# Two pools of slots re-divided: attention keys into the second pool, merged sums allocated at their first write

## The chip, the cores and the metric

The kernel runs on one core of a Trainium2 chip. The core's engines run side by side, each through its own queue of instructions in a fixed order: TensorE (PE in the profile, with its weight loads as PEld), VectorE (DVE), ScalarE (ACT), GpSimd (POOL), and SyncE (SP), which issues the transfers from memory. An instruction that has to wait holds up all that stand behind it on its engine. The metric is the device time of the run in microseconds; lower is better.

## The reference

Two transformer blocks run one after the other over 512 tokens of width 1024, batch 1, in fp32. The second block has two layers, and the change is in its mixing part, which four branches share. Cut to what matters:

```
h = rmsnorm(x); z = h @ w_in          # split: q, k, v of each branch, and 4 x 1024 gates
yA = forgetting_attention(qA, kA, vA, fA)    # 8 heads of 64, causal; logits + F[q] - F[k]
yB = dsa_attention(...)               # each query keeps its 128 best keys of an index score
yC = retention(...);  yD = sliding_window_gqa(...)
branch_n = y_n @ w_branch[n]          # 512 -> 1024
merged = sum over n of sigmoid(gates_n) * branch_n
x = x + merged @ w_out;  then a gated feed-forward layer
```

## The kernel before

Activations stand transposed, features on the 128 partitions and the 512 tokens along the row, so that a 1024-wide tensor is eight tiles of 128x512. fp32 products are made of three matmuls of rounded parts (mm3, L186 to L188): high by high, low by high, high by low. A weight block is loaded as `raw`, ACT rounds it to `hi` (L166), DVE subtracts to `lo` (L111). A product with 1024 inputs is 24 matmuls into one of four PSUM banks tagged `mm`; scores and transposes take three banks tagged `sc`, the product of probabilities and values one bank `pv`. A bank is free again when an engine has read it out.

SBUF tiles come from pools of equal slots of 128x512 fp32. `g` (L95) has 48 slots (NSLOT). `g2` (L100; its tiles are called h in the trace) has 12 (NSLOT2). A tile that is allocated while all slots are taken waits for the last reader of an older tile, so an instruction's first write to it can wait for an engine that has nothing to do with its data.

In `mix2` the slots of g2 go to `va`, the values of forgetting attention (4), to the eight tiles of `merged`, which are allocated ahead of everything else, and later to `vc` (4). In `fox_pair` each of four pairs of heads takes eight tiles of g: q, q2, k and k2, two each. Their scores are two matmuls each (L1116, L1117).

A pair's attention is a generator (`attend`) over four blocks c of 128 queries: scores on PE, mask and negative maximum on DVE (L1000), exponential on ACT (L123), reciprocal and scaling on DVE (L1012, L1014), transposes on PE (L1025), copies on ACT (L1028), and after the four blocks the product with the values on PE (L1039). The four pairs of forgetting attention, then four of the sparse branch (scores at L1128, L1129) stand in one list, `bg`; `pump` moves the first of them on by one step between two pieces of other work. A second list holds `select`, which finds the best 128 keys: 16 rounds of two DVE instructions (L1162, L1163) for each of three blocks, then L1168 makes the mask.

`branch` makes eight products of the gates (`gate(d)`, 24 matmuls each). A gate's bank is read out by a multiply on DVE (L111, out<-in `h<-psmm,g`) into `merged[d]` for the first branch, into a temporary tile for the others. With lead 4, gates 0 to 3 come first. Then the attention of the branch is drained, and the products with `w_branch` (12 matmuls for each of eight banks) take turns with gates 4 to 7. What is written is not what runs: a scheduler re-orders the program by priorities and free slots, and sets each engine's fixed order ahead of time.

Of the kernel before, what the change touches and what calls it, by code (L numbers as in the profile page):

```python
# [10 lines left out]
F32R = mybir.dt.float32r  # L11
# [9 lines left out]
KT = D // P  # L21
# [50 lines left out]
class Builder:  # L72
# [1017 lines left out]
    def fox_pair(self, ys, pair, pq, pk, va):  # L1090
        nc, ap = self.nc, self.ap
        tq, tk = self.tmp(), self.tmp()
        self.mul(tk, pk, self.rb)
        self.mul(tq, pq, self.rb)


        q, k = [self.g(F32R) for _ in range(2)], [self.g(F32R) for _ in range(2)]
        q2, k2 = [self.g(F32R) for _ in range(2)], [self.g(F32R) for _ in range(2)]
        hg, f0 = pair // 2, pair % 2 * 64
        fq, fk = self.fq[hg], self.fk[hg]  # L1100
        for i in range(2):
            r, o = slice(i * 64, i * 64 + 64), slice(64 - i * 64, 128 - i * 64)
            mine, other = 64 - i * 64 + i * 32, 64 - i * 64 + 32 - i * 32
            nc.scalar.copy(k[i][r], tk[r])
            nc.scalar.copy(k[i][o], tk[r])
            self.sub(k2[i][r], tk[r], k[i][r].bitcast(F32))
            nc.gpsimd.memset(k2[i][other:other + 32].bitcast(F32), 0.0)
            nc.scalar.copy(k2[i][mine:mine + 32], fk[f0 + i * 32:f0 + i * 32 + 32].bitcast(F32))
            nc.scalar.copy(q[i][r], tq[r])
            self.sub(q[i][o], tq[r], q[i][r].bitcast(F32))  # L1110
            nc.scalar.copy(q2[i][r], tq[r])
            nc.scalar.copy(q2[i][o], fq[f0:f0 + 64].bitcast(F32))

        def score(i, c, ps, k0, nk):
            qs = slice(c * P, (c + 1) * P)
            nc.tensor.matmul(ps, q[i][:, qs], k[i][:, k0:k0 + nk], start=True, stop=False)  # L1116
            nc.tensor.matmul(ps, q2[i][:, qs], k2[i][:, k0:k0 + nk], start=False, stop=True)  # L1117

        return self.attend(ys, pair, score, self.maskc, lambda i: 3e38,
                           lambda i, b: va[b][:, pair * P + i * 64:pair * P + i * 64 + 64],  # L1120
                           lambda c: list(range(c + 1)))
# [152 lines left out]
    def branch(self, l, n, y, x, first, gens=(), lead=3):  # L1274


        nc = self.nc
        gs = []

        def gate(d):  # L1280
            bk = self.bank("mm")
            self.gemm_b(bk, self.weights(self.I["w_gates"][l, n, d], KT * P), x)
            g = self.merged[d] if first else self.tmp()
            self.mul(g, bk, self.rb)
            self.act(g, g, AF.Tanh, scale=0.5)
            gs.append(g)
            self.pump(self.rate)

        for d in range(lead):
            gate(d)  # L1290
        self.drain(*gens)
        wb = None
        for d in range(KT):
            if d + lead < KT:
                gate(d + lead)
            if d % 2 == 0:
                wb = self.weights(self.I["w_branch"][l, n, d // 2], 1024)
            bb = self.bank("mm")
            self.gemm_b(bb, wb, [y[j] for j in range(4)], off=(d % 2) * 512)
            g = gs[d]  # L1300
            nc.vector.scalar_tensor_tensor(g, g, 1.0, bb, ALU.add, ALU.mult)
            if not first:
                self.add(self.merged[d], self.merged[d], g)
            self.pump(self.rate)
# [33 lines left out]
    def mix2(self, l):  # L1338
# [11 lines left out]
        self.cosR, self.sinR = self.g(), self.g()  # L1350
        self.mul(self.cosR, self.cload("cos"), self.rb)
        self.mul(self.sinR, self.cload("sin"), self.rb)
        self.merged = [self.g2() for d in range(KT)]
        proj = lambda n: self.rope(self.project(wr[n], x), self.tmp())

        hh, ll = self.stack_k(self.rope(b0, self.tmp()))
# [57 lines left out]
        for c in range(CHUNKS):  # L1414
            g = sg[c]
# [6 lines left out]
        q, k = [], []  # L1422
# [211 lines left out]
```

## Time and profile before

| | us |
|---|---|
| median of 3 runs (lowest, highest) | 3044.45 (3042.66, 3047.03) |
| profiled execution, own time | 3042.95 |
| its span, first to last instruction | 3041.1 |
| PE busy | 2962.3 |
| DVE busy | 1995.9 |

PE is busy for 97% of the span, so what can be saved or lost is mostly in its few idle stretches and in the stretches where its granted clock is below full. The clock has two levels, 1.2 and 2.4 GHz; the mean granted over the run is 0.989 of full. The mixing parts of the two layers lie at about 960 to 1600 us and 2020 to 2640 us, and the work that the change touches at about 1060 to 1180 and 2100 to 2220.

### The profile page before, as it was taken

The numbers are of one execution on the slowest core, as the hardware profiler recorded it, in microseconds if no ns is written. First come the engines' busy times: TensorE is split into PE (matmuls) and PEld (weight loads), VectorE is DVE, ScalarE is ACT, GpSimd is POOL, SyncE is SP. The second block draws the span as 40 slices with busy tenths as digits, with TensorE's granted clock in tenths as the row PEclk, the third lists the DMA queues.
The fourth block names the chain that finished last, engine by engine and source line by source line (L and its number), as shares of the span: only waits on it lengthen the run. The fifth ranks groups of instructions, "written<-read, shape, count | busy, mean of one in ns | idle before, by whom it ended". The sixth has DMA issues, their size and how long they took to land.

```text
span 3041.1 us, 38875 instructions
## 1 busy us (share of the span) xinstructions
PE 2962.3 (97%) x14882; PEld 2463.9 (81%) x14882; DVE 1995.9 (66%) x3866; ACT 1354.9 (45%) x2279; POOL 113.7 (4%) x148
## 2 busy tenths in 40 slices
PE   8999899999999998999999999999899999999998
PEld 7887888888888877887888888888687788888887
DVE  7888664545447796556666566659866467675575
ACT  5523443422226565545244333356655453343343
POOL 0000000011010000000000001000000000010010
PEclk9999999999999999999999999999999999999999
DMA  5224442233324221222243333332122222323322
GB/s 172 84 91 105 123 164 93 86 94 94 102 85 132 87 70 49 63 87 87 63 132 97 97 91 103 102 121 84 42 70 69 81 80 84 125 92 102 97 93 82
DMA packets 98395, 287.12 MB, mean 94 GB/s; under 512 B 12161, under 2 KB 20609, under 8 KB 98209
## 3 DMA queue, kind: packets, MB, share of 16 engines
q1 hardware_dynamic: 95744, 283.07, 30.1%
q10 hardware_dynamic: 2464, 1.57, 0.3%
q8 instruction: 117, 1.92, 0.3%
q14 instruction: 70, 0.57, 0.1%
HBM read 274.67 MB, written 9.93 MB: 94 GB/s over the span
## 4 chain that ended last, share of the span: by engine, by line
PE 90%; DVE 7%; ACT 2%; DMA 1%; issue 1%; ACTq 0%; SPq 0%; DVEq 0%
PE psmm L186 27%; PE psmm L187 27%; PE psmm L188 27%; PE pspv L1039 2%; PE pssc L1025 1%; DVE g L111 1%; DVE lo L111 1%; DVE g L1163 1%; DVE m L1162 1%; PE pssc L1128 1%; DVE tmp L111 1%; DVE prob L1000 1%; PE pssc L1129 1%; PE pspv L824 0%; PE pssc L792 0%
## 5 line engine op out<-in xcount | busy, mean ns | idle before, releaser
L186 PE MATMUL psmm<-g,hi 128*128 128x512 f32 (+1 forms) x3456 | 1342.9, 391 | 17.2 <-DVE h L111 6.4
L188 PE MATMUL psmm<-g,lo 128*128 128x512 f32 (+1 forms) x3456 | 1344.1, 390 | 3.5 <-DVE lo L111 3.5
L187 PE MATMUL psmm<-g,hi 128*128 128x512 f32 (+1 forms) x3456 | 1343.6, 389 | 0.0
L166 ACT CAST hi<-raw 128x1024 fp32r<-128x1024 f32 (+3 forms) x507 | 508.8, 1004 | 1157.7 <-PE psmm L187 827.7
L186 PEld LDWEIGHTS psmm<-g,hi 128*128 128x128 f32 x3456 | 650.2, 188 | 153.8 <-DVE g L111 5.1
L188 PEld LDWEIGHTS psmm<-g,lo 128*128 128x128 f32 x3456 | 650.7, 188 | 137.1 <-DVE lo L111 5.9
L187 PEld LDWEIGHTS psmm<-g,hi 128*128 128x128 f32 x3456 | 651.0, 188 | 129.4 <-issue 0.9
L111 DVE TENSOR_TENSOR lo<-raw,hi 128x1024 fp32r<-128x1024 f32 (+3 forms) x507 | 608.9, 1201 | 216.7 <-ACT hi L166 215.1
L111 DVE TENSOR_TENSOR tmp<-psmm,g 128x512 f32<-128x512 f32 x236 | 161.6, 688 | 287.7 <-PE psmm L188 275.3
L1480 DVE SCALAR_TENSOR_TENSOR g<-psmm,g 128x512 f32<-128x512 f32 x88 | 60.8, 691 | 150.0 <-PE psmm L188 150.0
L186 PE MATMUL psmm<-hi,g 128*128 128x512 f32 (+1 forms) x384 | 143.1, 379 | 10.5 <-ACT g L123 7.7
L111 POOL TENSOR_TENSOR tmp<-tmp,tmp 128x512 f32<-128x512 f32 x66 | 89.1, 1349 | 1522.1 <-DVE tmp L1454 520.9
L187 PE MATMUL psmm<-lo,g 128*128 128x512 f32 (+1 forms) x384 | 144.6, 377 | 0.0
L188 PE MATMUL psmm<-hi,g 128*128 128x512 f32 (+1 forms) x384 | 142.3, 373 | 0.0
L1454 DVE SCALAR_TENSOR_TENSOR tmp<-tmp,vec,tmp 128x510 f32<-128x510 f32 (+1 forms) x176 | 132.8, 757 | 2.5 <-ACT tmp L123 1.2
L111 DVE TENSOR_TENSOR g<-tmp,g 64x512 fp32r<-64x512 f32 (+2 forms) x166 | 113.4, 684 | 17.9 <-ACT g L166 11.0
L123 ACT ACTIVATE prob<-prob,nmx 128x128 f32<-128x128 f32 (+2 forms) x192 | 102.5, 535 | 46.1 <-DVE nmx L1000 41.6
L1028 ACT COPY probT<-pssc 128x128 f32<-128x128 f32 (+2 forms) x192 | 70.4, 399 | 76.8 <-PE pssc L1025 76.1
L1025 PE MATMUL pssc<-idn,prob 128*128 128x128 f32 x432 | 71.9, 286 | 24.3 <-DVE prob L1014 23.1
L123 ACT ACTIVATE tmp<-tmp 128x512 f32<-128x512 f32 (+1 forms) x138 | 84.1, 613 | 22.5 <-DVE tmp L111 18.0
L957 ACT COPY tmp<-psmm 32x512 f32<-32x512 f32 x160 | 92.4, 578 | 2.4
L186 PEld LDWEIGHTS psmm<-hi,g 128*128 128x128 f32 x384 | 73.0, 190 | 22.8 <-ACT g L123 7.7
(275 smaller groups left out, 2650.7 us busy)
## 6 DMA issues: line engine op xcount, KB each, us to landing
raw<-w_up SPq DMA_DIRECT2D x110, 512.0 KB, 3.5
raw<-w_gates SPq DMA_DIRECT2D x64, 512.0 KB, 3.5
raw<-w_down SPq DMA_DIRECT2D x72, 384.0 KB, 3.1
raw<-w_rope SPq DMA_DIRECT2D x40, 512.0 KB, 3.6
raw<-w_branch SPq DMA_DIRECT2D x32, 512.0 KB, 3.5
raw<-w_out SPq DMA_DIRECT2D x24, 512.0 KB, 3.5
raw<-w_gate SPq DMA_DIRECT2D x22, 512.0 KB, 3.6
raw<-w_fox SPq DMA_DIRECT2D x16, 512.0 KB, 3.4
```

The lines of the kernel that those rows point to most:

```text
L111: (eng or self.nc.vector).tensor_tensor(out, a, b, op)
L123: self.nc.scalar.activation(out, in_, func, **k)
L166: nc.scalar.copy(hi, src)
L186: mm(out, sh, mh, start=start, stop=False)
L187: mm(out, sh, ml, start=False, stop=False)
L188: mm(out, sl, mh, start=False, stop=stop)
L957: nc.scalar.copy(xs[k * 32:k * 32 + 32], bk[(k ^ 1) * 32:(k ^ 1) * 32 + 32])
L1025: nc.tensor.transpose(tr[:, j * P:(j + 1) * P], pt[i][:, j * P:(j + 1) * P], self.ident)
L1028: nc.scalar.copy(ptT, tr[:, :n * P])
L1039: nc.tensor.matmul(pv[i * 64:(i + 1) * 64, pc * P:(pc + 1) * P], value(i, b), tt[i][:, j * P:(j + 1) * P], start=j == 0, stop=j == len(bl) ...
L1454: nc.vector.scalar_tensor_tensor(o[:, sh:], u[:, :S - sh], w, o[:, sh:], ALU.mult, ALU.add)
L1480: self.nc.vector.scalar_tensor_tensor(self.x[d], ps, 0.5, self.x[d], ALU.mult, ALU.add)
```

## The change

Each pair's k and k2 (four tiles) come out of g2 instead of g. The eight tiles of `merged` are no longer allocated at the head of `mix2`; each is allocated from g2 inside `gate(d)` of the first branch, just ahead of the multiply that first writes it. The sizes of both pools stay. The number of instructions and their shapes stay as well.

```
-        q, k = [self.g(F32R) for _ in range(2)], [self.g(F32R) for _ in range(2)]
-        q2, k2 = [self.g(F32R) for _ in range(2)], [self.g(F32R) for _ in range(2)]
+        q, k = [self.g(F32R) for _ in range(2)], [self.g2(F32R) for _ in range(2)]
+        q2, k2 = [self.g(F32R) for _ in range(2)], [self.g2(F32R) for _ in range(2)]
...
-            g = self.merged[d] if first else self.tmp()
+            g = self.g2() if first else self.tmp()
+            if first:
+                self.merged.append(g)
...
-        self.merged = [self.g2() for d in range(KT)]
+        self.merged = []
```

So over time the 12 slots of g2 go to va (4), to the k tiles of two pairs (8), then of the next two, and only then to merged.

The order on PE moves in both layers alike. In layer 0, psmm_9740 of the order before and psmm_9735 of the order after are gate 3, psmm_9807 and psmm_9803 are gate 4. Before, PE at the end of gate 3:

```order
L187 MATMUL psmm_9740<-g_7777,hi_9743 128x512
L188 MATMUL psmm_9740<-g_7776,lo_9744 128x512
L186 MATMUL psmm_9807<-g_7710,hi_9810 128x512
L187 MATMUL psmm_9807<-g_7711,hi_9810 128x512
L188 MATMUL psmm_9807<-g_7710,lo_9811 128x512
L186 MATMUL psmm_9807<-g_7716,hi_9810 128x512
```

After the change, PE at the same place, and 52 rows further on:

```order
L187 MATMUL psmm_9735<-g_7777,hi_9738 128x512
L188 MATMUL psmm_9735<-g_7776,lo_9739 128x512
L1025 MATMUL pssc_8896<-idn_70,prob_8783 128x128
L1025 MATMUL pssc_8900<-idn_70,prob_8784 128x128
L1116 MATMUL pssc_8908<-h_8621,g_8619 128x384
...
L1116 MATMUL pssc_9380<-h_8837,g_8835 128x512
L1117 MATMUL pssc_9380<-h_8841,g_8839 128x512
L1116 MATMUL pssc_9384<-h_8838,g_8836 128x512
L1117 MATMUL pssc_9384<-h_8842,g_8840 128x512
L1025 MATMUL pssc_9393<-idn_70,prob_9303 128x128 x3
L186 MATMUL psmm_9803<-g_7710,hi_9806 128x512
```

Up to the end of gate 3 both orders hold the same instructions. Before, gate 4 follows at once. Now 57 rows of attention alone stand between the two (the rest of pair 1, its product with the values, and pair 2 up to its last block's scores, of bank pssc_9380 and its neighbour), and gates 4 to 7 and the branch products come behind them.

On DVE, before, a gate's multiply (h_7887, for gate 4) stands among the rounds of the selection (MAX, MATCH_REPLACE):

```order
L1014 TENSOR_SCALAR prob_8888<-prob_8888,sm_8890 128x256
L1163 MATCH_REPLACE g_8449<-m_1879_9072,g_8449 128x512
L111 TENSOR_TENSOR h_7887<-psmm_9807,g_7812 128x512
L1163 MATCH_REPLACE g_8259<-m_1880_9075,g_8259 128x256
L111 TENSOR_TENSOR lo_9942<-raw_9939,hi_9941 128x1024
L1163 MATCH_REPLACE g_8364<-m_1881_9078,g_8364 128x384
L111 TENSOR_TENSOR g_9040<-tmp_9036,g_9040 64x512
L1000 ISA prob_8912,nmx_8914<-pssc_8916,cst_1583_7842 128x384
```

After the change, DVE from the end of the selection (the mask L1168 of the longest block) to the first multiply into merged (h_9541, gate 0) and on:

```order
L1168 TENSOR_SCALAR g_8441<-g_8441 128x512
L111 TENSOR_TENSOR g_9209<-tmp_9161,g_9209 64x512
...
L1014 TENSOR_SCALAR prob_9232<-prob_9232,sm_9235 128x256
L1014 TENSOR_SCALAR prob_9233<-prob_9233,sm_9235 128x256
...
L1014 TENSOR_SCALAR prob_9303<-prob_9303,sm_9306 128x384
L1014 TENSOR_SCALAR prob_9304<-prob_9304,sm_9306 128x384
L111 TENSOR_TENSOR h_9541<-psmm_9510,g_7812 128x512
L1000 ISA prob_9376,nmx_9378<-pssc_9380,cst_1583_7842 128x512
L111 TENSOR_TENSOR h_9612<-psmm_9581,g_7812 128x512
L111 TENSOR_TENSOR h_9678<-psmm_9647,g_7812 128x512
```

All eight multiplies into merged stood ahead of the selection's last row before. Now none does, and the first stands directly ahead of the maximum of pair 2's last block (prob_9376), with the scaling of pair 2's blocks 1 and 2 (prob_9232, prob_9303) ahead of it. Its semaphore is PE's: the slot it writes held a k tile of pair 2, whose last reader is the score in bank pssc_9380. Both orders hold the same instructions again when the products with the third weight of `w_branch` begin.

## Rows read from the trace of the kernel before

**Rows 1.** the page: busy time of each engine over the span.
```profile
PE 2962.3 (97%) x14882; PEld 2463.9 (81%) x14882; DVE 1995.9 (66%) x3866; ACT 1354.9 (45%) x2279; POOL 113.7 (4%) x148
```

**Rows 2.** busy time by stretch: three of layer 0, three of layer 1.
```profile
core 0: us, PE busy (x) PEld busy (x) DVE busy (x) ACT busy (x) POOL busy (x), PEclk, DMA share, GB/s
1030.00:1096.30 66.30, 66.30 (x341) 55.32 (x340) 66.08 (x164) 44.18 (x79) 1.04 (x2) 1.00 0.26 80
1096.30:1137.00 40.70, 35.78 (x188) 28.37 (x187) 38.77 (x106) 26.42 (x56) 0.52 (x1) 0.96 0.24 79
1137.00:1177.70 40.70, 31.87 (x199) 26.26 (x198) 24.49 (x79) 24.58 (x67) 0.00 (x0) 0.83 0.00 0
2070.00:2136.30 66.30, 66.30 (x341) 55.29 (x341) 65.44 (x160) 45.31 (x81) 1.56 (x3) 1.00 0.28 88
2136.30:2177.00 40.70, 33.85 (x163) 26.89 (x163) 37.98 (x102) 25.01 (x51) 0.52 (x1) 0.93 0.21 65
2177.00:2220.10 43.10, 34.27 (x226) 28.33 (x223) 25.15 (x81) 25.51 (x69) 0.00 (x0) 0.87 0.00 1
```

**Rows 3.** PE waits, 1096.3 to 1177.7: total us, times, longest.
```profile
PE pssc L1025 <- DVE prob L1014: 8.6, 3, 4.2
```

**Rows 4.** PE in order of time at the marks: start, us, operation.
```profile
1095.65 0.39 PE L186 MATMUL psmm<-g,hi 128*128 128x512 f32 x1
...
1096.33 0.39 PE L186 MATMUL psmm<-g,hi 128*128 128x512 f32 x1
...
1177.66 0.40 PE L186 MATMUL psmm<-g,hi 128*128 128x512 f32 x1
...
2136.26 0.39 PE L186 MATMUL psmm<-g,hi 128*128 128x512 f32 x1
...
2220.13 0.40 PE L186 MATMUL psmm<-g,hi 128*128 128x512 f32 x1
```

**Rows 5.** DVE by shape, 1078.4 to 1132.5: count, busy us, mean ns, idle.
```profile
L111 DVE TENSOR_TENSOR lo<-raw,hi 128x1024 fp32r<-128x1024 f32 x8 | 9.7, 1210 | 0.0
...
L111 DVE TENSOR_TENSOR h<-psmm,g 128x512 f32<-128x512 f32 x8 | 5.4, 676 | 0.0
```

**Rows 6.** DVE in order of time: the selection's end, and pair 2.
```profile
1132.07 0.42 DVE L1168 TENSOR_SCALAR g<-g 128x512 f32<-128x512 f32 x1
1132.40 1.22 DVE L111 TENSOR_TENSOR lo<-raw,hi 128x1024 fp32r<-128x1024 f32 x1
1133.54 0.29 DVE L1000 CUSTOM_DVE_ANT_0 prob<-pssc,cst 128x128 f32<-128x128 f32 x1
...
1134.78 0.17 DVE L1012 RECIPROCAL sm<-sm 128x2 f32<-128x2 f32 x1 [0.74 <-ACT prob L123]
1134.98 0.48 DVE L1014 TENSOR_SCALAR prob<-prob,sm 128x128 f32<-128x128 f32 x2
1136.24 0.42 DVE L1000 CUSTOM_DVE_ANT_0 prob<-pssc,cst 128x256 f32<-128x256 f32 x1 [0.78 <-PE pssc L1117]
...
1137.66 1.41 DVE L111 TENSOR_TENSOR g<-tmp,g 64x512 fp32r<-64x512 f32 x2
1139.09 0.56 DVE L1000 CUSTOM_DVE_ANT_0 prob<-pssc,cst 128x384 f32<-128x384 f32 x1
...
2171.89 0.41 DVE L1168 TENSOR_SCALAR g<-g 128x512 f32<-128x512 f32 x1
```

**Rows 7.** PE in order of time: attention at either clock level.
```profile
1081.33 1.04 PE L1025 MATMUL pssc<-idn,prob 128*128 128x128 f32 x8
1082.12 0.31 PE L1116 MATMUL pssc<-g,g 128*128 128x128 f32 x1
...
1133.37 2.40 PE L1039 MATMUL pspv<-probT,h 128*64 128x128 f32 x38
...
1148.96 1.97 PE L1025 MATMUL pssc<-idn,prob 128*128 128x128 f32 x8 [4.24 <-DVE prob L1014]
...
1152.42 3.27 PE L1039 MATMUL pspv<-probT,h 128*64 128x128 f32 x38
```

## Prediction

> **What bounds the kernel now.** I read the page first: PE is busy for 2962.3 of 3041.1 us [rows 1], so little can be won, and the question is where the missing 79 us lie and what the change does there. Next the table by stretch [rows 2], for the part of either layer in which gates 0 to 7 of the first branch run beside the attention pairs. Up to 1096.3 PE and DVE are both full (66.30 and 66.08 of 66.30). From 1096.3 to 1177.7 PE is idle for 81.4 - 35.78 - 31.87 = 13.8 us, and the granted clock is 0.96 and 0.83 of full. With two levels, one half of the other, that is 8% of 40.7 and 34% of 40.7, or 3.3 + 13.8 = 17 us at the lower level. Layer 1 has the same picture (15.7 us idle, 0.93 and 0.87). Then what PE waits for there: mostly transposes waiting for DVE's scaling, 8.6 us in three waits [rows 3], which is the last stretch, where pairs 2 and 3 run with nothing beside them. In the first half, though, the full engine is DVE: 38.77 of 40.7 us, because the selection's rounds share it with everything else. PE has work there only because gates 4 to 7 stand in its queue.
>
> Two marks frame the sum. In layer 0 gate 3 ends and gate 4 begins at 1096.33; the third branch weight begins at 1177.66; in layer 1 the same marks are 2136.26 and 2220.13 [rows 4]. The orders hold the same instructions at either mark before and after the change, so all that counts is how long PE takes from the first to the second: 81.33 and 83.87 us now.
>
> **What the change does, in order.** It removes and adds no instruction; it moves slots. Gates 0 to 3 fill the four mm banks. Their multiplies into merged need slots of g2, and these are va's and the k tiles of pairs 2 and 3, once pairs 0 and 1 have handed theirs on. So the first multiply waits for pair 2's last score, gate 4 waits for the bank that this multiply frees, and PE's queue has only attention between gate 3 and gate 4 (57 rows in the order after). Four terms follow.
>
> *When the first multiply runs.* DVE works off its queue in order and is full, so its queue gives the time. In the trace the selection's last row starts at 1132.07 and ends for the next at 1132.40 [rows 6]. Compared with what stood ahead of that row, DVE has less to do ahead of the first multiply: all eight multiplies (8 x 0.676 = 5.4 us) and three of the subtractions to lo (3 x 1.21 = 3.6 us) now come later [rows 5]. It has more: pair 2's maxima for blocks 0 to 2, two heads each, 2 x (0.29 + 0.42 + 0.56) = 2.5; three reciprocals, 0.5; scalings of three blocks, 0.48 for the narrowest two and my estimate 1.8 in all; eight subtractions for the sparse branch's queries, two in 1.41, so 5.6; one subtraction after pair 1's values, about 0.7 [rows 5, 6]. That is 11.1 - 9.0, about +2.1; by start to start, where neighbours overlap by some 0.08 us, it is nearer 2.6. I take 2.4. The multiply starts at 1134.8, in layer 1 at 2171.89 + 0.33 + 2.4 = 2174.6, and ends 0.6 later. The 38 us that PE spends from 1096.33 to there hold only some 10 us of its work.
>
> *New waits on DVE.* With the selection over, pair 2's steps show: before, the reciprocal waited 0.74 and the next block's maximum 0.78 [rows 6]. Behind DVE's waiting row stand the multiply and the next lo. I take 1.2 us; at least 0, at most 4 (each of the pair's steps waits like that).
>
> *Work left for PE.* Behind gate 4's start stand four gates and two branch weights, 96 + 48 = 144 matmuls at (1096.33 - 1095.65) / 3 = 0.227 us [rows 4], 32.7; two products with values, 80 matmuls at 2.40 / 38, 5.1; 37 transposes at 0.79 / 8 (from 1081.33 to the next start at 1082.12), 3.7 [rows 7]; 30 score matmuls between 0.10 and 0.227, say 0.18, 5.4. The sum is 46.8 us at the full clock; DVE's and ACT's staging of a gate's weights (1.21 us on DVE) hides beside its 24 x 0.227 = 5.4 us.
>
> *What this refill loses.* The upper clock is gone after a long idle: after 4.24 us without work the eight transposes at 1148.96 took 1.97 us instead of 1.04, and the product behind them 3.27 instead of 2.40 [rows 7]. The refill begins the same way, with dense work; I take 3 us, at least 0, at most the 7 us that half of 13.8 us at the lower level costs. Gate 6 waits for pair 3's last score in its turn, since the banks are then held by gates 4 and 5 and two unfinished branch products: 1.5 us idle, from 0 to the 8.6 us that PE waited before.
>
> Layer 0: 1134.8 + 0.6 + 1.2 + 46.8 + 3 + 1.5 = 1187.9, 10.2 us after 1177.66. Layer 1: 2174.6 + 53.1 = 2227.7, 7.6 after 2220.13. Nothing behind the marks gives it back: there PE has its matmuls in the same order and is full. Ahead of the first mark I cost the changed order at nothing; PE's 66.30 busy of 66.30 us covers it, and without that cover it would be a wait or two of DVE's size, 1 us. Sum: +17.8 on the profiled execution's 3042.95 (span 3041.1 and 1.85 around it), 3060.8, said as **3061 us**. That execution stands 1.5 us below the median of 3044.45, so it could as well be read 3062.
>
> **Rivals.** *The refill is free:* no wait, full clock, no idle. Then layer 0 ends at 1134.8 + 0.6 + 46.8 = 1182.2 and layer 1 at 2222.0, together +6.4: 3049. For it speaks that gates and attention are mixed finely in the new order; against it rows 7, and that DVE's next maxima stand behind multiplies that wait for PE.
>
> *The refill limps:* the clock stays low as long as before (7 us lost) and each held bank costs the old 8.6 us of idle. That adds 4 + 7.1 = 11 us per layer, 3083. Against it: dense gates now stand where PE had nothing.
>
> *The other side: relieved slots fill the holes.* Pairs 2 and 3 leave PE idle in the last stretch, and the new order puts 21.8 us of gates there. If the first multiply came soon enough, those gates would run in time that is now lost. It decides at 1177.66 - 46.8 - 4.5 - 0.6 = 1125.8 for the first multiply in layer 0: any earlier and the change gains, at most the 13.8 + 15.7 us of idle and some 12 of clock, 3001; if a third of that came back, 3029. Against it stands DVE's queue, which alone takes until 1134.8, 9 us too late. The Trainium skill, on the page "Perfetto Trace Analysis", section "Optimization Strategy", reads a gap that repeats on the engine that should be full as a possible shortage of room for the next tile; by that rule a better division of the slots would close the holes and the time would be near the 3001. The trace does not agree: the waits of [rows 3] name DVE's scaling and no slot, and the room for merged is what gets scarce.
>
> *It does nothing:* the orders differ in just this place, so I give that no chance of its own.
>
> **How the numbers follow.** Forecast 0.70, limping refill 0.11, free refill 0.12, other side 0.07. The forecast's own range, 5 us to either side per layer for waits, clock and idle together, is 3051 to 3071. What a measurement of this kernel can tell is 0.2%, 6.1 us, so "same" reaches to 3050.5: the free refill and a little of the rest. Faster 0.07, same 0.13, slower 0.80. The range for 8 in 10 leaves out the far ends of both sides: 3047 to 3079.
>
> **What would show it.** Right: from about 1096 to 1136 PE is idle for more than 20 us, its waits naming DVE's scaling or maxima and its granted clock well below 0.96; the first `h<-psmm` multiply comes between 1134 and 1139, after the selection; then both PE and clock are full to about 1187; the same in layer 1, with the end some 18 us later. Wrong: a first multiply before 1126, gates among the selection's rounds, or PE idle again for more than 6 us between gate 4 and the third branch weight.

## The result, and the profile after

The changed kernel takes 3061.76 us (median of 4 runs, 3061.51 to 3063.12), the kernel before 3044.13 us beside it: a ratio of 1.0055, 95% interval 1.0043 to 1.0067, or 13 to 20 us more. The forecast of 3061 us was met. The profiled run after has a span of 3061.3 us, 20.2 more than before.

The times by stretch of the kernel after answer to [rows 2]; the stretches are cut where gate 3 ends, where gate 4 begins and where the third branch weight begins, in layer 0 and then in layer 1:

```profile
core 0: us, PE busy (x) PEld busy (x) DVE busy (x) ACT busy (x) POOL busy (x), PEclk, DMA share, GB/s
1030.00:1098.80 68.80, 68.80 (x351) 56.96 (x349) 68.23 (x167) 48.00 (x86) 1.04 (x2) 1.00 0.27 85
1098.80:1139.50 40.70, 19.77 (x94) 14.57 (x94) 39.52 (x117) 24.82 (x60) 1.03 (x2) 0.62 0.04 14
1139.50:1187.90 48.40, 48.30 (x293) 39.45 (x293) 25.43 (x70) 25.01 (x60) 0.00 (x0) 1.00 0.15 44
...
2148.30:2189.70 41.40, 20.07 (x94) 15.21 (x94) 38.19 (x111) 24.99 (x61) 1.03 (x2) 0.64 0.04 13
2189.70:2239.10 49.40, 49.30 (x294) 40.14 (x293) 25.35 (x70) 25.44 (x61) 0.00 (x0) 0.99 0.14 43
```

Before, PE's idle time was spread over both halves of the stretch. Now it lies in the first alone (40.70 - 19.77 = 20.9 us), and the second is full. Over both halves of layer 0, PE is busy for 68.07 us (67.65 before) and idle for 21.0 (13.8 before); in layer 1 for 69.37 (68.12) and 21.4 (15.7). So the loss between the marks is idle time, 7.3 + 5.8 us, and 1.7 us of slower work.

PE's waits of the kernel after in the stretch of layer 0, beside [rows 3] (total us, times, longest):

```profile
PE pssc L1025 <- DVE prob L1014: 16.2, 5, 6.5
PE pssc L1116 <- ACT probT L1028: 4.0, 1, 4.0
```

No row of PE names a slot or a bank here. Gate 4 stands behind pairs 1 and 2 in PE's queue, and each wait is put down to the attention row at its head. The slot shows on DVE only. In time order, DVE and then PE of the kernel after (start, us, operation, in brackets the wait and what ended it):

```profile
1128.59 0.42 DVE L1168 TENSOR_SCALAR g<-g 128x512 f32<-128x512 f32 x1
1129.03 2.12 DVE L111 TENSOR_TENSOR g<-tmp,g 64x512 fp32r<-64x512 f32 x3
...
1131.78 3.56 DVE L111 TENSOR_TENSOR g<-tmp,g 64x512 fp32r<-64x512 f32 x5
...
1138.04 0.69 DVE L111 TENSOR_TENSOR h<-psmm,g 128x512 f32<-128x512 f32 x1 [0.38 <-PE pssc L1116]
1138.65 0.68 DVE L1000 CUSTOM_DVE_ANT_0 prob<-pssc,cst 128x512 f32<-128x512 f32 x1
```
```profile
1098.52 0.39 PE L188 MATMUL psmm<-g,lo 128*128 128x512 f32 x1
1105.16 0.69 PE L1025 MATMUL pssc<-idn,prob 128*128 128x128 f32 x2 [6.25 <-DVE prob L1014]
...
1117.61 1.51 PE L1025 MATMUL pssc<-idn,prob 128*128 128x128 f32 x6 [6.51 <-DVE prob L1014]
1119.68 1.97 PE L1025 MATMUL pssc<-idn,prob 128*128 128x128 f32 x8 [0.56 <-DVE prob L1014]
...
1139.51 0.48 PE L186 MATMUL psmm<-g,hi 128*128 128x512 f32 x1
...
1187.91 0.39 PE L186 MATMUL psmm<-g,hi 128*128 128x512 f32 x1
...
2148.05 0.39 PE L188 MATMUL psmm<-g,lo 128*128 128x512 f32 x1
...
2189.73 0.78 PE L186 MATMUL psmm<-g,hi 128*128 128x512 f32 x1
...
2239.06 0.39 PE L186 MATMUL psmm<-g,hi 128*128 128x512 f32 x1
```

The first multiply into merged waits for a score of line 1116, that of pair 2's last block (the maximum behind it at 1138.65 reads it). Gate 4 begins 1.47 us later, its first matmul with 0.48 us in layer 0 and 0.78 in layer 1 (0.39 in [rows 4]). Eight transposes in the stall took 1.97 us, as those behind a long gap in [rows 7].

### The profile page after: what moved, and what is told of

Same layout as the page of the kernel before. It is cut to its first block, busy times and chain, and to the rows that moved or that the text cites. A ratio compares the mean times of both kernels' runs of the same rounds, so it can differ in the third digit from the quotient of the medians.

```text
span 3061.3 us, 38897 instructions
## 1 busy us (share of the span) xinstructions
PE 2967.6 (97%) x14882; PEld 2465.8 (81%) x14882; DVE 1995.6 (65%) x3866; ACT 1354.3 (44%) x2279; POOL 114.1 (4%) x148
## 4 chain that ended last, share of the span: by engine, by line
PE 91%; DVE 7%; DMA 1%; ACT 1%; issue 1%; ACTq 0%; SPq 0%; DVEq 0%
PE psmm L186 27%; PE psmm L188 27%; PE psmm L187 27%; PE pspv L1039 2%; PE pssc L1025 1%; DVE g L111 1%; DVE g L1163 1%; DVE lo L111 1%; DVE m L1162 1%; DVE prob L1000 1%; PE pssc L1128 1%; DVE tmp L111 1%; PE pssc L1129 0%; DMA raw<-w_down 0%; PE pspv L824 0%
## 5 line engine op out<-in xcount | busy, mean ns | idle before, releaser
L111 DVE TENSOR_TENSOR g<-tmp,g 128x512 fp32r<-128x512 f32 (+2 forms) x150 | 102.5, 685 | 18.2 <-ACT g L166 11.0
L1025 PEld LDWEIGHTS pssc<-idn,prob 128*128 128x128 f32 x432 | 56.5, 150 | 63.2 <-DVE prob L1014 28.0
```

The costliest lines, as they stand in the source:

```text
L111: (eng or self.nc.vector).tensor_tensor(out, a, b, op)
L1025: nc.tensor.transpose(tr[:, j * P:(j + 1) * P], pt[i][:, j * P:(j + 1) * P], self.ident)
```

## The experiments

The theory at the start: the k tiles hold g2's slots, so the first multiply waits for pair 2's last score, and DVE's full queue sets when that comes. Each kernel ran in several rounds beside the kernel before on the same chip (medians of before there: 3042.95 to 3044.45), and the ratio is to that. The last two columns are read from PE's rows in time order: from gate 0's first matmul to the third branch weight, in layer 0 and 1.

| kernel | median us | ratio to before, 95% | layer 0 | layer 1 |
|---|---|---|---|---|
| before | 3044.13 | | 108.1 | 110.7 |
| changed | 3061.76 | 1.0043 to 1.0067 | 116.0 | 117.7 |
| merged late, k as before | 3043.74 | 0.9990 to 1.0007 | 108.5 | 110.8 |
| k in g2, merged as before | 3060.83 | 1.0041 to 1.0066 | 116.0 | 117.7 |
| change in layer 0 only | 3053.30 | 1.0018 to 1.0039 | 116.3 | 113.0 |
| 47 and 13 slots | 3055.74 | 1.0023 to 1.0050 | 113.5 | 113.1 |
| 46 and 14 slots | 3055.40 | 1.0027 to 1.0055 | 115.7 | 111.4 |
| 46, 16 slots, 8 tmp | 3070.10 | 1.0075 to 1.0104 | 114.8 | 108.4 |
| one slot apart | 3059.30 | 1.0039 to 1.0066 | 113.8 | 113.4 |
| three slots apart | 3050.95 | 1.0013 to 1.0033 | 110.0 | 109.9 |
| before, 8 rounds | 3026.55 | 0.9931 to 0.9957 | 101.4 | 100.6 |
| changed, 8 rounds | 3045.57 | 0.9996 to 1.0014 | 109.4 | 110.1 |
| lo on GpSimd, 28 per layer | 3052.11 | 1.0018 to 1.0039 | 107.2 | 108.7 |
| lo on GpSimd, 8 per layer | 3042.69 | 0.9989 to 1.0007 | 108.3 | 109.3 |

**Either part alone.** Merged allocated late, k left in the first pool:

```
-        q, k = [self.g(F32R) for _ in range(2)], [self.g2(F32R) for _ in range(2)]
+        q, k = [self.g(F32R) for _ in range(2)], [self.g(F32R) for _ in range(2)]
```
(and the same for q2, k2)

> One part of the change alone: the tiles of merged are allocated when first written, the k tiles stay in the first pool. Theory (the k tiles hold the slots that merged needs; the first multiply into merged is late because of that): with the k tiles away, g2 holds merged and va as before, the order of PE's rows is that of the kernel before, and the time is too: 3044, within 3 us. Rival (the late allocation itself costs, since a multiply then waits for a slot): some or all of the 17.6 us, 3053 to 3062.

And the other part, k in g2 with merged allocated at the layer's start:

```
-        self.merged = []
+        self.merged = [self.g2() for d in range(KT)]
...
-            g = self.g2() if first else self.tmp()
+            g = self.merged[d] if first else self.tmp()
```
(and without the two lines that append to merged)

> The other part alone: forgetting attention's k tiles in the second pool, merged allocated at the layer's start as before. Theory: a slot is needed from a tile's first write on, wherever it was allocated, so this is the whole change: 3062, 17 us above before, with the first multiply into merged at about 1136 to 1138 us in layer 0. Rival (both parts are needed for the loss): 3044 to 3053.

Measured: 3043.74 and 3060.83. The late allocation costs nothing; the k tiles are the whole change. PE's 14882 rows, compared by operation, names and shapes, stand in the order of the kernel before in the first and in that of the changed kernel in the second. In the k-only kernel gate 4 and the third branch weight begin, on PE:

```profile
1138.55 0.48 PE L186 MATMUL psmm<-g,hi 128*128 128x512 f32 x1
...
1186.91 0.39 PE L186 MATMUL psmm<-g,hi 128*128 128x512 f32 x1
```

That is the changed kernel's picture, 1 us earlier throughout. Where merged is allocated in the program made no difference; its slots are needed from its first write.

**One layer.**

```
+        kk = self.g2 if self.l == 0 else self.g
-        q, k = [self.g(F32R) for _ in range(2)], [self.g2(F32R) for _ in range(2)]
+        q, k = [self.g(F32R) for _ in range(2)], [kk(F32R) for _ in range(2)]
```
(merged allocated late in layer 0 alone, too)

> The change in layer 0 alone; layer 1 as before. The trace after the change shows 7.8 us lost between the marks of layer 0 and 6.9 between those of layer 1, and some 4 us outside both. Theory (the loss is made at the two stalls): about 3044 + 8 = 3052, at most 3055; layer 1 between its marks as before, 83.9 us. Rival (part of the 17.6 us is made elsewhere, by a shift of everything behind): if a layer-independent cost of about 3 us comes with it, 3055 to 3057; if the loss is in the other layer, 3044.

Measured: 3053.30, half the loss, with layer 0 at 116.3 as in the full change. Layer 1, whose order on PE is that of before row by row, took 2.3 us more than before, though. Its two halves:

```profile
2145.60:2186.30 40.70, 33.88 (x163) 26.91 (x163) 37.97 (x102) 25.01 (x51) 0.52 (x1) 0.94 0.22 65
2186.30:2231.80 45.50, 37.51 (x227) 31.65 (x224) 25.30 (x81) 25.80 (x69) 0.00 (x0) 0.79 0.00 1
```

PE is idle for 14.8 us, not more than the 15.7 of before, but busy for 71.4 instead of 68.1, at a granted clock of 0.79 in the second half instead of 0.87. So one and the same order of PE can take 2 or 3 us more or less by where the clock falls, and the price of a layer is known no better than that.

**More slots in g2.** One and two slots moved from the first pool:

```
-NSLOT = 48
-NSLOT2 = 12
+NSLOT = 47
+NSLOT2 = 13
```

> The changed kernel with one slot moved from the first pool to the second (47 and 13 instead of 48 and 12). Theory: one tile of merged finds a free slot, so gate 0 leaves its bank at once and gate 4 runs in the stall (24 matmuls, 5.4 us of PE's work moved into idle time); the next multiply still waits for pair 2. The loss falls by about 5 us per layer, 3044 + 18 - 10 = 3051 (3046 to 3055). Rival (the loss comes from the new mixture of gates and pairs, or from DVE's queue, and no slot matters): 3058 to 3064.

> The changed kernel with two slots moved from the first pool to the second (46 and 14). Theory: gates 0 and 1 leave their banks at once, gates 4 and 5 run ahead of pair 2's last scores, and the rest of the gates stands among pairs 2 and 3, where the kernel before left PE idle for 13.8 and 15.7 us. The loss is gone and some of those holes are filled: 3036 (3030 to 3046). Rival (no slot matters): 3058 to 3064.

Measured: 3055.74, just above the expected 3046 to 3055, and 3055.40 where 3036 was expected: a miss. Stretches of layer 0 with 13 slots, cut at gate 4's start and end and 2.7 us into gate 5, which starts at 1140.07; then two rows of DVE and gate 4's first row of PE:

```profile
1099.30:1116.70 17.40, 5.27 (x15) 3.02 (x14) 17.17 (x51) 11.01 (x27) 1.03 (x2) 0.61 0.10 31
1116.70:1125.20 8.50, 8.45 (x36) 6.90 (x37) 8.50 (x28) 1.82 (x4) 0.00 (x0) 0.79 0.01 2
1125.20:1142.80 17.60, 11.82 (x74) 8.58 (x73) 17.00 (x44) 13.85 (x33) 0.00 (x0) 0.75 0.09 30
1142.80:1185.80 43.00, 42.63 (x265) 34.82 (x264) 20.82 (x64) 21.28 (x55) 0.00 (x0) 0.98 0.12 37
```
```profile
1114.11 0.66 DVE L1000 CUSTOM_DVE_ANT_0 prob<-pssc,cst 128x512 f32<-128x512 f32 x1
...
1116.01 0.69 DVE L111 TENSOR_TENSOR h<-psmm,g 128x512 f32<-128x512 f32 x1
...
1116.76 0.79 PE L186 MATMUL psmm<-g,hi 128*128 128x512 f32 x1 [5.08 <-DVE h L111]
```

Here a row does name the multiply: gate 4 waits for it. The first multiply does not come at once: it follows pair 1's last maximum, 17 us after gate 3. I had expected a free slot; what it fits is that pair 2 takes the added slot, and the first tile of merged gets one of pair 1's (inferred, not shown; with 14 slots the first multiply follows pair 1's last maximum too, at 1118.46). PE is idle before gate 4 as it was, and the next gate waits for pair 2. With 14 slots the first two multiplies come at 1119.9 and 1121.0 and the third at 1144.0.

The same with four slots more in g2, two of them from the first pool and two for two temporaries:

```
-NSLOT = 48
-NSLOT2 = 12
-NTMP = 10
+NSLOT = 46
+NSLOT2 = 16
+NTMP = 8
```

> The changed kernel with 46 slots in the first pool, 16 in the second and 8 temporaries instead of 10. Theory: four tiles of merged find free slots, gates 4 to 7 need wait for no score; as with 14 slots or a little better, unless the two temporaries are missed: 3035 (3028 to 3048). Rival (no slot matters): 3058 or more.

Measured: 3070.10, outside the expected range. Layer 1's stretch is shorter than in the kernel before (108.4), but the kernel loses elsewhere, for example 10.7 us more than the kernel before between the third branch weight of layer 0 and gate 0 of layer 1 (942.5 against 931.8). In layer 0 the first multiply comes at 1114.85, 13.5 us after gate 3's end, and the stretch is 114.8: there the added slots were no more free for merged than one or two were. The two temporaries may be the loss elsewhere; they were not tried apart.

**DVE's load.** Half the selection, in the kernel before and in the changed one; both leave out the rest of the keys:

```
-        for r in range(16):
+        for r in range(8):
```

> The kernel before with 8 rounds of selection instead of 16 (it keeps 64 keys a row instead of 128). It is the partner of the next run. DVE has 48 instructions fewer per layer, some 24 us of its queue. Both theories: a little faster than before, since pairs 2 and 3 are less delayed, 3034 (3026 to 3042).

> The changed kernel with 8 rounds of selection instead of 16 (64 keys a row). Theory (the first multiply into merged is late because DVE's full queue delays pair 2, and that alone makes the loss): the multiply comes some 15 to 20 us sooner after gate 3's end than in the changed kernel, ahead of the break-even of 29.5 us after the mark (1125.8 against 1096.3), so this is not slower than its partner, and by the filled holes some us faster: 3028, from 8 us below the partner to equal. Rival (the loss is the price of fewer slots or of the new order whatever DVE does): 3052, some 17 us above the partner.

Measured: 3026.55 and 3045.57. The partner gained more than expected, 17 us. But the changed kernel is 19.0 us slower than its partner, as the rival said: the theory's number fell. The changed kernel with 8 rounds, by stretch and on DVE:

```profile
1095.80:1129.00 33.20, 18.55 (x94) 13.98 (x93) 21.25 (x56) 24.52 (x58) 1.06 (x2) 0.65 0.05 17
1129.00:1178.20 49.20, 49.12 (x294) 39.95 (x293) 25.34 (x70) 25.15 (x61) 0.00 (x0) 0.99 0.14 43
```
```profile
1127.49 0.69 DVE L111 TENSOR_TENSOR h<-psmm,g 128x512 f32<-128x512 f32 x1 [0.51 <-PE pssc L1116]
```

DVE is busy for only 21.25 of 33.2 us, and still the multiply waits for pair 2's last score until 31.6 us after gate 3's end (39.1 with 16 rounds). So halving the selection takes 7.5 us off the delay, and the kernel before gains by it as well (101.4 for 108.1 us in layer 0). What stays is for one thing pair 2's own way: score, maximum, exponential, scaling, transpose, and the next block again. For another it is the order of DVE's queue, whatever its load. Between pair 2's maxima for its third block (the last at 1119.69) and the scaling of its second block stand seven subtractions for the sparse branch's queries, and PE waits meanwhile (DVE, then PE):

```profile
1120.29 3.56 DVE L111 TENSOR_TENSOR g<-tmp,g 64x512 fp32r<-64x512 f32 x5
...
1124.07 1.40 DVE L111 TENSOR_TENSOR g<-tmp,g 64x512 fp32r<-64x512 f32 x2
1125.51 0.62 DVE L1014 TENSOR_SCALAR prob<-prob,sm 128x256 f32<-128x256 f32 x2
...
1125.91 1.11 PE L1025 MATMUL pssc<-idn,prob 128*128 128x128 f32 x4 [7.15 <-DVE prob L1014]
```

The changed kernel has eight of them ahead of that scaling (the rows at 1129.03 and 1131.78 above), the kernel before four. What the change would cost with them behind it was not run. So these two runs show that the change costs as much at half the selection's load; whether the order of DVE's rows is part of the cost they leave open.

The last maxima of pairs 1, 2 and 3 come at 1120.09, 1144.03 and 1162.05 in the kernel before, at 1113.46, 1140.45 and 1163.67 in the changed one. From gate 3's end, pair 1 is then 9 us ahead of before, but pair 2 only some 6 us, although PE had nothing else beside it; pair 3 is 0.8 us ahead.

**One and three slots apart.** The theory revised: the pairs go at nearly their own pace whether PE has gates beside them or not, and gates taken from there are missing later. So what counts is how many gates find a slot before pair 2.

```
-NSLOT = 48
+NSLOT = 45
...
+    def own(self):
+        return self.ap.tile([P, S], F32, name=self.nm("own"), tag="own", bufs=3)
...
-            g = self.g2() if first else self.tmp()
+            g = (self.own() if d < 3 else self.g2()) if first else self.tmp()
```
(for one slot 47, bufs=1 and d < 1)

> The changed kernel with a slot of its own, free from the start, for the first tile of merged (47 slots in the first pool, 12 in the second, 1 apart). Revised theory (the pairs go at a pace that their own chain and DVE set: pair 2's last maximum comes only 6 us sooner when four gates and more are taken away from beside the pairs, and those gates' PE time is missing at the end): gate 0 leaves its bank at once, gate 4 runs right behind gate 3 at the full clock, and 5.5 us less is left after the stall; pair 2 comes 1 to 2 us later for it. The third branch weight begins some 4 us later than in the kernel before per layer, 3044 + 8 = 3052 (3048 to 3056), a little better than the 3055.7 of the 47/13 slots, where gate 4 ran at the low clock. Rival (the slot that merged 0 gets is no matter, only the new order of the pairs): 3058 to 3064.

> The same with three slots apart (45, 12 and 3), for merged 0, 1 and 2: gates 4 and 5 and the first products run right behind gate 3. Revised theory: 11 us and a bit of PE's work back beside pair 1, pair 2's last score 3 us later than in the changed kernel; what is left then takes about as long as pair 3's own chain, so the third branch weight begins about where it did before: 3044 (3038 to 3050). If the two gates left fill pair 3's holes, 3038; if the 45 slots of the first pool are too few, above 3050. Rival (as for one slot): 3058 to 3064.

Measured: 3059.30 and 3050.95, each above its range, but the stretch moves as expected: 113.8 and 113.4, then 110.0 and 109.9, against 108.1 and 110.7 before. With three slots apart, 219.9 us in both layers stand against 218.8 before and 233.7 after the change: nearly all of the loss in these two stretches is back, though 8.0 us of the 17.6 in the whole kernel are not. Layer 0 of that kernel, with gates 4 and 5 run at once:

```profile
1103.20:1114.90 11.70, 11.68 (x52) 9.17 (x51) 11.51 (x29) 6.26 (x15) 0.00 (x0) 1.00 0.14 46
1114.90:1142.00 27.10, 14.73 (x86) 10.84 (x84) 26.82 (x82) 17.16 (x38) 1.30 (x2) 0.73 0.13 39
1142.00:1186.30 44.30, 40.72 (x248) 33.16 (x249) 25.63 (x76) 24.20 (x66) 0.00 (x0) 0.90 0.07 24
```

What the total lacks lies outside: its gate 0 of layer 0 begins at 1076.32, 6.8 us later than before, with three slots fewer in the first pool. Part of this is scatter between profiles (the changed kernel: 2.4 us later, merged late: 1.9 earlier, in unchanged order), so what the lost slots cost is not settled; the kernel before with 45 slots was not run. With one slot apart, too, only 8.4 of the profile's 17.0 us over the kernel before lie in the two stretches.

**A way to less DVE.** The halved selection showed that DVE's time in the stretch is worth something to either kernel. In the kernel before, GpSimd was given the subtraction for staged weights, first from the selection's start on, then from gate 4 on:

```
             nc.scalar.copy(hi, src)
-            self.sub(lo, src, hi.bitcast(F32))
+            self.sub(lo, src, hi.bitcast(F32), eng)
...
+            self.lo_eng = nc.gpsimd if first and d >= 4 else None
```
(the last line is the second kernel's; the first sets `lo_eng` where the selection starts)

> The kernel before, with the subtraction that makes lo of each staged weight on GpSimd instead of DVE, from the selection's start to the end of the first branch (28 per layer). DVE's selection costs time (8 rounds fewer made the kernel before 17 us faster, for 96 instructions of DVE), so DVE's queue is a price by itself, apart from slots. Theory: 28 x 1.21 = 34 us of DVE's queue less per layer; if half of it stands in the stretch that DVE fills, by the rate of the 8 rounds (17 us for some 48 us of DVE) 2 x 17 x 17 / 48 = 12 us gained, 3032 (3026 to 3040). Rival (GpSimd, whose 128x512 product takes 1.35 us against DVE's 0.68, delays the weights, so that PE waits for lo): 3048 or more.

> The kernel before, with the subtraction that makes lo on GpSimd only for the weights of gates 4 to 7 and the four branch weights of the first branch, eight per layer; nothing ahead of gate 4 is moved. In the run with 28 such subtractions the time from gate 0 to the third branch weight fell by 1.0 and 2.0 us although gates 0 to 3 were 4 to 5 us later; here they keep their places. Theory (DVE's queue sets the pace of pairs 1 and 2 in this stretch; 8 rounds of selection fewer, some 24 us of DVE per layer, gave 8.4 us per layer): 8 x 1.21 = 9.7 us of DVE gives 0.35 x 9.7 = 3.4 us per layer, 3043.5 - 7 = 3037 (3032 to 3042). Rival (the work on GpSimd makes other engines slower or weights late): 3043 to 3052, as with 28.

Measured: 3052.11, slower, and 3042.69, no difference (0.9989 to 1.0007); the theory's numbers failed both times. (The first kernel's profile, and so its two stretches in the table, is of its fastest run, 3042.90.) GpSimd and DVE in the second kernel, layer 0:

```profile
L113 POOL TENSOR_TENSOR lo<-raw,hi 128x1024 fp32r<-128x1024 f32 x8 | 19.5, 2438 | 157.3 <-ACT hi L168 157.3
```
```profile
1095.10:1137.00 41.90, 36.69 (x194) 29.18 (x194) 34.37 (x95) 27.41 (x59) 12.74 (x6) 0.96 0.23 76
```

DVE is relieved (34.37 of 41.90 us), yet PE's stretch is 108.3 us as before. Of the kernels that keep all 16 rounds, none was clearly faster than the one before.

## Why the prediction was right

The marks of the trace after lie 2.42 us later than before at gate 3's end in layer 0 and 12.02 in layer 1; the numbers here are less that.

- *When the first multiply runs.* Forecast 1134.8 and 2174.6; measured 1138.04 - 2.42 = 1135.6 and 2188.19 - 12.02 = 2176.2. The count of DVE's rows was right to 0.8 and 1.6 us, and the eight subtractions that it put ahead of the multiply stood there. What it stood for was not the whole reason: with half the selection the multiply comes 7.5 us sooner and the change costs as much. Pair 2's own chain and the order of DVE's rows, which stay, end little earlier than the full queue does; the forecast named the queue alone.
- *New waits on DVE.* Forecast 1.2 us. The waits ahead of the multiply are 0.38 and 0.51; gate 4 began at 1137.1 in layer 0, forecast 1136.6, and at 2177.7 in layer 1, forecast 2176.4. Right in sum to 0.5 and 1.3 us.
- *Work left.* Forecast 46.8 us; PE was busy for 48.3 in layer 0 and 49.3 in layer 1. The forecast was 1.5 and 2.5 short.
- *What the refill loses.* Forecast 3 us of clock and 1.5 of idle; measured a clock of 1.00 and 0.99 and 0.1 us of idle in either layer. This is the term that was mis-sized: of 4.5 us nothing came. The clock was low in the stall (0.62), where little work stood, and full again when the dense gates began. In this the rival "the refill is free" was right; its 3049 fell, because in layer 0 the multiply came 0.8 us later than it had it, gate 4 another 0.9 and the work was 1.6 longer.
- *The sum.* Between the marks 7.8 and 6.9 us, forecast 10.2 and 7.6: 14.7 instead of 17.8. That the 17.6 us between the medians lie so close to the forecast is luck in part: the 3.1 us too many were made up by what it put at nothing. Of the 20.2 us between the two profiles, 2.4 lie ahead of layer 0's first mark, 1.8 between the layers (1.6 of them at one place, below) and 1.3 behind layer 1; profiles scatter by 2 us ahead of the marks. The forecast held PE's order behind the marks for the same. It is not quite: some rows behind the third branch weight are exchanged. That costs nothing: a matmul there at 1219.1 us before runs at 1229.3 after, still 10.2 us later, as at the mark.
- *The other side.* The break-even of 1125.8 was never reached: 1135.6. The kernels with slots apart show the mechanism, though: gates in the first half give the loss back. The holes of [rows 3] were not filled in any run with more slots: with three slots apart PE is idle for 16.0 us between the marks of layer 0 (13.8 before). The Trainium skill, page "Perfetto Trace Analysis", section "Optimization Strategy", reads a repeated gap on the engine that should be full as a possible lack of room. For the new gap the runs agree: k in g2 alone makes it, three slots for merged take it away. For the holes that the kernel before had they don't, as far as they go: with k and more slots in g2 at most 2.3 us of one layer's stretch was gained (108.4 for 110.7). More slots for g2 with k in the first pool were not run.

The kernel before has idle time in the same stretch: it lasts 81.4 us and holds 67.65 us of PE's work, and PE waits for the pairs' scalings [rows 3]. The change moved some 21.8 us of gates from beside pairs 1 and 2 to beside pair 3. Pair 2 came 6 us sooner for it, and PE then had more left than pair 3 could cover.

## What to carry to other kernels

In this program a tile's slot counts from its first write, so ask which last reader frees it and what stands in the producer's queue behind that. The gap shows under another name: the consumer's wait is put down to whatever row heads its queue. When filler is moved in a stretch that a chain of dependent steps bounds, count how much sooner the chain ends without the filler; if that is less than the filler's time, the move costs the difference. Before halving a load to prove a cause, run the same halving without the change, for it may be worth as much there.

## What the runs showed of the hardware

**The same gap, another clock.** In either layer, some 200 us behind the stretch, PE waits 2.28 to 2.29 us for one scaling, in every trace of this case. Ten microseconds around it in layer 0 of the kernel before and of the changed one:

```profile
1380.00:1390.00 10.00, 7.28 (x61) 5.75 (x60) 7.42 (x30) 6.81 (x21) 0.00 (x0) 1.00 0.16 55
```
```profile
1390.20:1400.20 10.00, 7.27 (x52) 5.91 (x50) 5.84 (x24) 5.23 (x17) 0.00 (x0) 0.83 0.19 55
```

PE is busy equally long, but the clock is 1.00 in the one and 0.83 in the other, which then gets 9 matmuls less done and is 1.6 us behind. The kernels with k in g2 alone and with layer 0 alone changed show the fall (0.61 and 0.60 in the 4 us behind the gap), as does the changed kernel with 8 rounds (0.83); merged late and the kernel before with 8 rounds show none there. In layer 1 the kernel before shows the fall as well:

```profile
2422.50:2432.50 10.00, 7.27 (x53) 5.76 (x51) 5.85 (x24) 5.29 (x18) 0.00 (x0) 0.83 0.18 52
```

So the same gap is followed by a fall or by none even within one kernel; what decides it was not found. Layer 1 of the kernel with layer 0 alone changed may be another such place: no more idle time, but a lower clock.

**GpSimd.** The 128x1024 subtraction took 2.44 us there, 1.21 on DVE [rows 5]. The runs of these two kernels lie further apart than those of before: 3042.9 to 3056.4 and 3038.3 to 3049.5 us, against 3041.4 to 3046.7; their profiled runs were at the fast end. The longer runs have the lower mean clock (0.986 and 0.987 in those above 3050 us, 0.990 in the one of 3042.9); what lowers it, no run here shows.
